# A two-stack transformer on one core: activations at other offsets to the weights in SBUF, and the forget decay of the keys added on VectorE instead of by a matmul

## The chip, the cores and the metric

The kernel runs on one core of a Trainium2 chip. The metric is the device time of one execution in microseconds (us), lower is better; the median of three executions is given. Five engines work side by side on the core: TensorE (PE, with its weight loads listed as PEld), VectorE (DVE), ScalarE (ACT), GpSimd (POOL) and SyncE (SP), which here only issues DMAs.

## The reference

256 tokens of width 1024 go through two stacks of two layers each. The first stack has three attention-like branches and a gated feed-forward network in each layer; the second has two feed-forward networks around a mixer. Nearly all of the arithmetic is `x @ w` with a weight matrix that is read once. The part of the reference beside these products that the change touches is the forgetting attention of the first stack:

```python
def forgetting_attention(q, k, v, f_logit):
    log_f = jax.nn.log_sigmoid(f_logit)
    cum = jnp.cumsum(log_f, axis=1).transpose(0, 2, 1)      # 4 heads x 256 tokens
    for blk in range(s // Q_BLOCK):                         # Q_BLOCK = 128
        ...
        logits = jnp.einsum('bihd,bjhd->bhij', q[:, q0:q1], k[:, :q1]) * d ** -0.5
        logits = logits + cum[:, :, q0:q1, None] - cum[:, :, None, :q1]
        mask = jnp.arange(q0, q1)[:, None] >= jnp.arange(q1)[None, :]
        p = jax.nn.softmax(jnp.where(mask, logits, -jnp.inf), axis=-1)
        ...
```

The term `- cum[:, :, None, :q1]` belongs to the key; it is the same for all queries.

## The kernel before, in words

The activations lie transposed, features on partitions and tokens along the free dimension, as 8 (or 22) blocks `k` of 128 features by 256 tokens. Every fp32 operand of a large product is split into a high and a low part (`hh`, `hl` for the activations, `wh`, `wl` for the weights), and `mm3` (lines 332 to 337) makes one product of three matmuls: `wh`·`hh`, `wh`·`hl` and `wl`·`hh`. The activations move, 256 columns long, and the 128x128 piece of the weights is loaded. In `kT` (line 354) the roles are exchanged. There are 15,600 of these matmuls.

`run` (line 259) takes the weights in the order of the program's steps: SP loads 512 KB into one of six `raw` tiles, ACT makes `wh` (line 289) and DVE makes `wl` (line 290) from half of it, four halves ahead of the matmuls. One half feeds twelve matmuls. The tiles `wh` and `wl` have ten buffers each of 2048 bytes per partition, and each starts at 128 modulo 256 bytes.

The activations lie as follows, as the program's addresses give it. The distance is the start of the activation operand less the start of the weight operand of the same matmul, modulo 256 bytes; it is the same for all blocks and for the high and the low tile, except where the table has a list.

| operand, where | matmuls | distance before |
|---|---|---|
| `hh`, `hl` (norm's output, xp pool) | 8,208 | 0 |
| `hidh`, `hidl` (hidden layer of a feed-forward network) | 3,168 | 128 |
| `bh`, `bl` where no norm is due (`norm_begin(None)`), rows of 258 tokens | 2,112 | 0, 8, ... 56 in `bh`, 64, 72, ... 120 in `bl`, by block |
| `brh`, `mxh`, `yh`, `ph` and their low parts | 1,248 | 128 |
| `bh`, `bl` in `first_pair` with a norm, 258 columns | 864 | 0 to 56 and 64 to 120, by block |

The forgetting attention: `small` (line 927) makes the cumulative sums `cum` of four heads as four rows and their negative `ncum`. Four units of the input projection later, `cores` (line 1157) flushes what is deferred and starts `fox(h)` for the four heads, five ticks apart (a tick is one block `k` of a large product). `fox` (line 950) writes the scores of two query blocks into PSUM with two plain fp32 matmuls, and adds `ncum` of its head to all rows with two more, whose loaded operand is one column of the identity matrix broadcast to 128 columns of four rows (`selh`). Each plain fp32 matmul shows as two records in the trace. DVE then adds the query's `cum` and the mask in one instruction for each query block (lines 960 and 961), and ACT and DVE make the softmax. Other work of PE goes on between the parts of `fox`.

Of the kernel before, what the change touches and what calls it, by code (L numbers as in the profile page):

```python
# [15 lines left out]
S = 256  # L16
# [5 lines left out]
NEG = -1e30  # L22
# [31 lines left out]
def _consts():  # L54
    f = np.float32
    ident = np.eye(128, dtype=f)
    half = 64
    inv = (f(10000.0) ** (-np.arange(half, dtype=f) / f(half))).astype(f)
    ang = (np.arange(S, dtype=f)[:, None] * inv[None, :]).astype(f)
    cos = np.cos(ang.astype(np.float64)).astype(f).T  # L60
    sin = np.sin(ang.astype(np.float64)).astype(f).T
    cosF = np.concatenate([cos, cos], 0)
    sinF = np.concatenate([-sin, sin], 0)
    i = np.arange(128)
    foxm = np.concatenate([np.zeros((128, 128), f),
                           np.where(i[:, None] >= i[None, :], 0.0, NEG).astype(f)], 1)
    u = ((i[:, None] > i[None, :]) & (i[:, None] // 64 == i[None, :] // 64)).astype(f)
    sel = (i[:, None] // 64 == np.arange(2)[None, :]).astype(f)
    t = np.arange(S)
    retd = []  # L70
    for h in range(4):
        lg = np.log1p(-np.exp2(-5.0 - h))
        d = np.exp(np.abs(t[:, None] - t[None, :]) * lg) * 128.0 ** -0.5
        d = np.where(t[:, None] // 64 <= t[None, :] // 64, d, 0.0).astype(f)
        retd += [d[:128], d[128:, 128:]]
    retd = np.concatenate(retd, 1)
    dist = np.abs(t[:, None] - t[None, :]).astype(f)
    ci, cj = t[:, None] // 64, t[None, :] // 64
# [113 lines left out]
class Prog:  # L192
# [6 lines left out]
    def __init__(self, ctx, tc, io, dbg=None):  # L199
        self.tc, self.nc, self.io, self.dbg = tc, tc.nc, io, dbg  # L200
        nc = self.nc
        self.V, self.A, self.G, self.PE = nc.vector, nc.scalar, nc.gpsimd, nc.tensor
        self.steps = []
        self.side = []
        pool = lambda name, **k: ctx.enter_context(tc.tile_pool(name=name, **k))
        self.cp = pool("cst", bufs=1)
        self.wp = pool("wts", bufs=self.WB)
        self.xp = pool("res", bufs=1)
        self.np_ = pool("nrm", bufs=2)
        self.tp = pool("tiny", bufs=4)  # L210
        self.dp = pool("dram", bufs=1, space=bass.MemoryType.DRAM)
        self.pg = pool("psg", bufs=4, space=PSUM)
        self.pm = pool("psm", bufs=4, space=PSUM)
        self.off, npar = _offsets()
        self.par = self.cp.tile([128, npar], F32, name="par")
        self.ident = self.cp.tile([128, 128], F32, name="ident")
        self.ones = self.cp.tile([128, 256], F32, name="ones")
        self.mhalf = self.cp.tile([128, 16], F32, name="mhalf")
        self.mod = [self.cp.tile([128, 48], F32, name=f"mod{l}") for l in range(2)]
        self.cact = self.np_.tile([128, D], F32, name="cact", tag="sy", bufs=1)  # L220
        self.gm = {}
        self.x = self.xp.tile([128, 8, S], F32, name="x")
        for k in (0, 4):
            self.dma(self.x[:, k:k + 4, :], io["xT"].rearrange("p (k t) -> p k t", t=S)[:, k:k + 4, :])
        self.dma(self.cact, io["cb"])
        self.dma(self.par, io["par"])
        self.dma(self.ident, io["c_id"])
        self.V.memset(self.ones, 1.0)
        self.V.memset(self.mhalf, -0.5)
        self.lam = self.cp.tile([128, 8], F32, name="lam")  # L230
        self.A.activation(self.lam[:, 0:1], self.mhalf[:, 0:1], AF.Silu)
        self.A.activation(self.cact, self.cact, AF.Silu)
# [179 lines left out]
    def norm_begin(self, kind, a=None, b=None):  # L412
# [4 lines left out]

        bh = self.xp.tile([128, 8, S + 2], F32R, name="bh", tag="bh")
        bl = self.xp.tile([128, 8, S + 2], F32R, name="bl", tag="bl")
        nk = {"kind": kind, "bh": bh, "bl": bl}  # L420
        if kind == "rms":
            base = 24 * b
# [17 lines left out]
                gains(o, 4)  # L440
        nk["gains"] = gains
        self.nk = nk

    def norm_add(self, mp, **k):
        with self.tc.high_priority():
# [81 lines left out]
    def norm_apply_(self):  # L527

        nk, V, A, x = self.nk, self.V, self.A, self.x
        bc = nk["bc"]  # L530
        hh = self.xp.tile([128, 8, S], F32R, name="hh", tag="hh")
        hl = self.xp.tile([128, 8, S], F32R, name="hl", tag="hl")
        qv, qa = self.queue(), self.queue(1)
        if nk["kind"] == "ln":
            parts = [slice(0, 1), slice(1, 2)] if 0 else [slice(0, 2)]
# [81 lines left out]
    def opening(self, units):  # L617


        def stats(ws):  # L620
            self.h = tuple(self.xp.tile([128, 8, S], F32R, name=n, tag=n) for n in ("hh", "hl"))
            g = self.tp.tile([128, 8], F32, name="gm", tag="gm")
            self.nk = {"kind": "rms", "bh": None, "bl": None, "g": g, "b": self.mod[0][:, 0:8]}
            for mp in range(4):
                self.norm_add(mp, split=False)
            self.norm_stats()
            self.norm_spread()
            self.opened = self.nk["spread"]
# [82 lines left out]
    def ffn_first(self, l, extra=()):  # L711
# [2 lines left out]
        st = {}  # L714

        def begin(ws):
            st["hh"] = self.st([128, KF, S], F32R, "hidh")
            st["hl"] = self.st([128, KF, S], F32R, "hidl")
        self.step([], begin)
        wc, bc = f"w_conv{l}", f"b_conv{l}"  # L720

# [51 lines left out]
    def ffn_second(self, l, f, j_ln):  # L773
# [1 line left out]
        st = {}  # L775

        def begin(ws):
            st["hh"] = self.st([128, KF, S], F32R, "hidh")
            st["hl"] = self.st([128, KF, S], F32R, "hidl")
        self.step([], begin)  # L780

        def evac_g(j):
# [87 lines left out]
    def mix(self, l, extra=()):  # L870
# [18 lines left out]
        self.step([], begin)  # L889

        def tables(ws):
            c = T([128, 898 + 1536], F32, "cmix")
            self.dma(c, self.io["c_mix"])
            b["cos"], b["sin"], b["foxm"] = c[:, 0:256], c[:, 256:512], c[:, 512:768]
            b["U"], b["sel"] = c[:, 768:896], c[:, 896:898]
            b["retd"] = c[:, 898:898 + 1536].rearrange("p (h c) -> p h c", h=4)
            a2 = T([128, 256], F32, "a2")
            self.dma(a2[32:49, :], self.io[f"a2{l}"][32:49, :])
            b["a2"] = a2


        def fox_qk(dst, u, gi):
            def fn(ps):
                if u == 0:
                    b[dst] = T([128, 4, S], F32, dst)
                n = self.st([128, 4, 128], F32, "w2", 4)
                r = self.head_rs(ps.rearrange("p t (h d) -> p (t h) d", h=2), 4, "hr")
                V.tensor_tensor(out=n, in0=ps.rearrange("p t (h d) -> p (t h) d", h=2),
                                in1=r[:, 0:4].unsqueeze(2).to_broadcast([128, 4, 128]), op=MULT)

                def turn():
                    pt = self.psM((128, 2, S))
# [14 lines left out]
        def small(ps):  # L927
# [8 lines left out]
            cum = z  # L936
            V.tensor_tensor_scan(out=cum[0:4, :], data0=self.ones[0:4, :], data1=lf[0:4, :], initial=0.0, op0=MULT, op1=ADD)
            V.tensor_scalar(lf[0:4, :], cum[0:4, :], -1.0, None, MULT)
            b["ncum"] = lf

            def turn():
                pt = self.psM()
# [4 lines left out]
                V.tensor_copy(out=b["cumT"], in_=pt[:, 0:8])  # L947
            self.defer(12, turn)

        def fox(h):  # L950
            q, k, v, m = b["qF"], b["kF"], b["fv"], b["foxm"]
            ps = self.psM((128, 2, S))
            mm = lambda o, l_, r_, s, e: PE.matmul(o, l_, r_, start=s, stop=e, skip_group_check=True)  # L953
            selh = self.ident[0:4, h:h + 1].to_broadcast([4, 128])
            for t in range(2):
                n = 128 * (t + 1)
                mm(ps[:, t, 0:n], q[:, h, t * 128:(t + 1) * 128], k[:, h, 0:n], t == 0, False)
                mm(ps[:, t, 0:n], selh, b["ncum"][0:4, 0:n], False, True)
            s = T([128, 384], F32, "sc", 2)
            V.scalar_tensor_tensor(s[:, 0:128], ps[:, 0, 0:128], b["cumT"][:, h:h + 1], m[:, 128:256], ADD, ADD)  # L960
            V.scalar_tensor_tensor(s[:, 128:384], ps[:, 1, :], b["cumT"][:, 4 + h:5 + h], m, ADD, ADD)
            nm = self.tiny(2, "nm")
            V.tensor_reduce(out=nm[:, 0:1], in_=s[:, 0:128], axis=AX.X, op=MAX, negate=True)
            V.tensor_reduce(out=nm[:, 1:2], in_=s[:, 128:384], axis=AX.X, op=MAX, negate=True)
# [191 lines left out]
            self.one(wi(5), keepT("fv", 1), "T")  # L1156
        def cores(ws):
            self.flush()
            self.spawn(gla_decay())
            for h in range(4):  # L1160
                self.spawn(fox(h), 5 * h)
            self.tick(0)
# [346 lines left out]
    def mixer_c(self, l):  # L1509
# [399 lines left out]
        def ybuf(ws):  # L1909
            while "cored" not in b:  # L1910
                self.tick()
            b["yh"] = self.xp.tile([128, 8, S], F32R, name="hh", tag="hh")
            b["yl"] = self.xp.tile([128, 8, S], F32R, name="hl", tag="hl")
            for hp in b["early"]:
                ysplit(hp)

# [73 lines left out]
```

## Time and profile before

| | |
|---|---|
| median of three runs (lowest to highest) | 2081.24 us (2081.13 to 2082.68) |
| the profiled execution | 2082.02 us |
| its span, first to last instruction | 2080.2 us |
| PE busy | 2033.9 us (98%) |
| DVE, ACT, POOL busy | 1534.7 us (74%), 1202.1 us (58%), 43.0 us (2%) |
| mean granted clock of PE | 0.997 of full speed |
| read from HBM | 397.32 MB |

Busy time of PE is the union of the matmuls' records. A record lasts some 280 ns and the next one begins after 120 ns, so records overlap, and "98%" does not tell how fast the matmuls follow each other. For that one counts the records in a stretch.

### The profile page before, as it was taken

The page shows a single profiled execution, that of the slowest core. Times are in us where ns is not written, and L with a number is a line of the kernel's source. Part 1 is how long each engine was busy: PE and PEld are TensorE (multiplying, and loading weights), DVE is VectorE, ACT ScalarE, POOL GpSimd, SP SyncE. Part 2 cuts the span into 40 slices and gives each one's busy share as a digit, 9 for nine tenths or more (in the row PEclk, how much of TensorE's full clock was granted, in tenths as well). Part 3 has the DMA queues.
Part 4 walks back from the last instruction along what each step waited for, and adds up shares of the span by engine and source line. Part 5 has one row for each costly group of instructions (what it writes and reads, how often), then busy time and mean ns, then how long its engine had stood idle before and what let it go on. Part 6 is the DMA issues. An engine that isn't in the chain of part 4 may idle for free.

```text
span 2080.2 us, 42885 instructions
## 1 busy us (share of the span) xinstructions
PE 2033.9 (98%) x16848; PEld 2006.6 (96%) x16848; DVE 1534.7 (74%) x2971; ACT 1202.1 (58%) x2255; POOL 43.0 (2%) x46
## 2 busy tenths in 40 slices
PE   7999999999999999999999999999999999899998
PEld 7999999999999999999999999999999998899998
DVE  8768989977669789765566898567755687586557
ACT  4755466566645467554555777556655586365545
POOL 0000000000000000000000000000000000000000
PEclk9999999999999999999999999999999999999999
DMA  9746977875447877666656346664656654246553
GB/s 340 248 121 199 322 250 243 293 239 193 144 156 245 277 243 243 193 178 189 186 180 190 127 131 208 184 180 156 211 184 180 180 156 127 62 147 200 179 168 103
DMA packets 123488, 403.40 MB, mean 194 GB/s; under 512 B 17010, under 2 KB 24468, under 8 KB 123028
## 3 DMA queue, kind: packets, MB, share of 16 engines
q1 hardware_dynamic: 112868, 397.24, 60.0%
q10 hardware_dynamic: 10416, 3.41, 0.6%
q8 instruction: 132, 2.16, 0.4%
q14 instruction: 72, 0.59, 0.1%
HBM read 397.32 MB, written 3.28 MB: 193 GB/s over the span
## 4 chain that ended last, share of the span: by engine, by line
PE 91%; DVE 5%; DMA 2%; issue 1%; POOL 1%; ACT 1%; DVEq 0%; ACTq 0%; POOLq 0%
PE psg L334 26%; PE psg L335 26%; PE psg L336 26%; PE psw L334 1%; PE psw L335 1%; PE psw L336 1%; DVE wl L290 1%; DMA raw<-w_ada 1%; PE psm L1687 1%; PE psm L953 1%; PE psm L1782 1%; DMA xx<-dx 1%; DMA dx<-xb 1%; PE psm L409 0%; PE psm L1084 0%
## 5 line engine op out<-in xcount | busy, mean ns | idle before, releaser
L289 ACT CAST wh<-raw 128x512 fp32r<-128x512 f32 x1304 | 783.7, 616 | 668.3 <-PE psg L335 467.6
L290 DVE TENSOR_TENSOR wl<-raw,wh 128x512 fp32r<-128x512 f32 x1304 | 871.9, 684 | 363.7 <-ACT wh L289 345.9
L334 PE MATMUL psg<-hh,wh 128*128 128x256 f32 x2328 | 661.8, 285 | 3.6 <-ACT wh L289 3.2
L335 PE MATMUL psg<-hl,wh 128*128 128x256 f32 x2328 | 661.5, 284 | 1.5 <-DVE hl L388 1.4
L336 PE MATMUL psg<-hh,wl 128*128 128x256 f32 x2328 | 661.0, 284 | 0.8 <-DVE wl L290 0.8
L334 PEld LDWEIGHTS psg<-hh,wh 128*128 128x128 f32 x2328 | 447.0, 192 | 5.8 <-ACT wh L289 3.5
L335 PEld LDWEIGHTS psg<-hl,wh 128*128 128x128 f32 x2328 | 447.9, 192 | 2.3 <-DVE hl L388 1.6
L336 PEld LDWEIGHTS psg<-hh,wl 128*128 128x128 f32 x2328 | 447.7, 192 | 1.5 <-DVE wl L290 1.0
L336 PE MATMUL psg<-hidh,wl 128*128 128x256 f32 x1056 | 297.3, 282 | 0.0
L335 PE MATMUL psg<-hidl,wh 128*128 128x256 f32 x1056 | 297.3, 282 | 0.0
L334 PE MATMUL psg<-hidh,wh 128*128 128x256 f32 x1056 | 297.3, 282 | 0.0
L334 PEld LDWEIGHTS psg<-hidh,wh 128*128 128x128 f32 x1056 | 198.9, 188 | 0.0
L335 PEld LDWEIGHTS psg<-hidl,wh 128*128 128x128 f32 x1056 | 198.8, 188 | 0.0
L336 PEld LDWEIGHTS psg<-hidh,wl 128*128 128x128 f32 x1056 | 198.8, 188 | 0.0
L335 PE MATMUL psg<-bl,wh 128*128 128x256 f32 x704 | 197.9, 281 | 0.0
L336 PE MATMUL psg<-bh,wl 128*128 128x256 f32 x704 | 197.8, 281 | 0.0
L334 PE MATMUL psg<-bh,wh 128*128 128x256 f32 x704 | 197.7, 281 | 0.0
L402 DVE CUSTOM_DVE_ANT_0 raw<-raw,cact,par 128x1024 f32<-128x1024 f32 x96 | 122.5, 1279 | 29.9 <-DMA raw<-w_ada 29.9
L335 PEld LDWEIGHTS psg<-bl,wh 128*128 128x128 f32 x704 | 132.8, 189 | 0.3 <-DVE bl L388 0.2
L334 PEld LDWEIGHTS psg<-bh,wh 128*128 128x128 f32 x704 | 132.8, 189 | 0.0
L336 PEld LDWEIGHTS psg<-bh,wl 128*128 128x128 f32 x704 | 132.6, 188 | 0.0
L334 PE MATMUL psg<-wh,hh 128*128 128x256 f32 (+1 forms) x336 | 97.7, 294 | 0.0
(446 smaller groups left out, 3004.7 us busy)
## 6 DMA issues: line engine op xcount, KB each, us to landing
raw<-f_up SPq DMA_DIRECT2D x176, 512.0 KB, 4.5
raw<-w_ada SPq DMA_DIRECT2D x96, 512.0 KB, 5.2
raw<-w_up SPq DMA_DIRECT2D x88, 512.0 KB, 5.1
raw<-f_dn SPq DMA_DIRECT2D x80, 512.0 KB, 3.7
raw<-w_in SPq DMA_DIRECT2D x66, 512.0 KB, 4.0
raw<-w_mg SPq DMA_DIRECT2D x46, 512.0 KB, 5.0
raw<-w_down SPq DMA_DIRECT2D x40, 512.0 KB, 4.2
raw<-c_in SPq DMA_DIRECT2D x32, 512.0 KB, 4.5
```

Of the source, the lines that this page charges most:

```text
L289: self.A.copy(out=wh[:, :e], in_=r)
L290: self.V.tensor_tensor(out=wl[:, :e], in0=r, in1=wh[:, :e].bitcast(F32), op=SUB)
L334: mm(ps, wh, xh, start=first, stop=False, skip_group_check=True)
L335: mm(ps, wh, xl, start=False, stop=False, skip_group_check=True)
L336: i = mm(ps, wl, xh, start=False, stop=last, skip_group_check=True)
L402: i = self.V.tensor_tensor_reduce(out=w, in0=w, in1=self.cact, scale=1.0, scalar=self.P(f"b_ada{l}", j), op0=MULT, op1=ADD, accum_out=self ...
L953: mm = lambda o, l_, r_, s, e: PE.matmul(o, l_, r_, start=s, stop=e, skip_group_check=True)
L1687: mm = lambda o, l_, r_, s: PE.matmul(o, l_, r_, start=s, stop=True, skip_group_check=True)
L1782: PE.matmul(p[:, i, :], l_(i, h), r_(i, h), start=(i == 0), stop=True, skip_group_check=True)
```

## The change

Two edits that don't depend on each other, and a small one.

1. The tiles `hh`/`hl` get 256 bytes more, `hidh`/`hidl` 512, and `pair_of` puts the data inside them at an offset from a table, one number for each stage. All distances are then the same for the high and the low tile. `bh`, `bl` without a norm are packed to rows of 256.

| stage, in order | operand | before | after |
|---|---|---|---|
| layer 0: mixing, then feed-forward | `hh` | 0 | 64, 192 |
| | `hid` | 128 | 192 |
| layer 1: mixing, then feed-forward | `hh` | 0 | 192, 224 |
| | `hid` | 128 | 224 |
| second stack, layer 0 | packed `bh`, `bl` | 0 to 120, mixed | 0 and 64 |
| | `hid` (two networks) | 128 | 64, 160 |
| | `hh` (mixer, second network, gate) | 0 | 64, 32, 192 |
| second stack, layer 1 | packed `bh`, `bl` | 0 to 120, mixed | 0 and 64 |
| | `hid` (two networks) | 128 | 32, 96 |
| | `hh` (mixer in, mixer out, second network, gate) | 0 | 160, 64, 128, 64 |

Four of the `hh` stages (the feed-forward ones) have 960 matmuls each, every `hid` stage has 528.

2. `ncum` is written to DRAM by POOL's queue (4x256) and read back spread over 128 partitions (128x1024, 512 KB). Ahead of `fox`, `fox_bias` adds the mask to it, one half in a tile `nb0`, one half in place. `fox` leaves out its two matmuls with `selh`, and DVE adds the prepared tile where it added the mask. The table `c_mix` shrinks by 128 columns.

```diff
+        self.places = [b // 4 for b in (64, 192, 192, 224, 64, 32, 192, 160, 64, 128, 64)]
+        self.hid_places = [b // 4 for b in (64, 96, 192, 32, 160, 224)]
...
+        if kind is None:
+            bh, bl = (t.rearrange("p k t -> p (k t)")[:, 0:8 * S].rearrange("p (k t) -> p k t", t=S) for t in (bh, bl))
...
+    def pair_of(self, pool, tag, kt, extra, at):
+
+        out = []
+        for n in (tag + "h", tag + "l"):
+            t = pool.tile([128, kt * S + extra], F32R, name=n, tag=n, bufs=1)
+            out.append(t[:, at:at + kt * S].rearrange("p (k t) -> p k t", t=S))
+        return tuple(out)
+
+    def normed(self):
+
+        return self.pair_of(self.xp, "h", 8, 64, self.places.pop(0))
...
-        hh = self.xp.tile([128, 8, S], F32R, name="hh", tag="hh")
-        hl = self.xp.tile([128, 8, S], F32R, name="hl", tag="hl")
+        hh, hl = self.normed()
...
-            st["hh"] = self.st([128, KF, S], F32R, "hidh")
-            st["hl"] = self.st([128, KF, S], F32R, "hidl")
+            st["hh"], st["hl"] = self.pair_of(self.sp, "hid", KF, 128, self.hid_places.pop(0))
...
-            b["ncum"] = lf
+            nd = self.dp.tile([4, S], F32, name=f"nd{l}")
+            nb = b["nb"] = T([128, 4, S], F32, "sall")
+            self.nc.gpsimd.dma_start(out=nd, in_=lf[0:4, :])
+            self.nc.gpsimd.dma_start(out=nb, in_=nd.unsqueeze(0).to_broadcast([128, 4, S]))
...
+        def fox_bias():
+
+            m = b["foxm"].unsqueeze(1).to_broadcast([128, 4, 128])
+            b["nb0"] = T([128, 4, 128], F32, "w2", 4)
+            with self.tc.issue_after(b["normed"]):
+                V.tensor_tensor(out=b["nb0"], in0=b["nb"][:, :, 0:128], in1=m, op=ADD)
+            with self.tc.issue_after(b["normed"]):
+                V.tensor_tensor(out=b["nb"][:, :, 128:256], in0=b["nb"][:, :, 128:256], in1=m, op=ADD)
...
-            selh = self.ident[0:4, h:h + 1].to_broadcast([4, 128])
             for t in range(2):
                 n = 128 * (t + 1)
-                mm(ps[:, t, 0:n], q[:, h, t * 128:(t + 1) * 128], k[:, h, 0:n], t == 0, False)
-                mm(ps[:, t, 0:n], selh, b["ncum"][0:4, 0:n], False, True)
+                mm(ps[:, t, 0:n], q[:, h, t * 128:(t + 1) * 128], k[:, h, 0:n], t == 0, True)
             s = T([128, 384], F32, "sc", 2)
-            V.scalar_tensor_tensor(s[:, 0:128], ps[:, 0, 0:128], b["cumT"][:, h:h + 1], m[:, 128:256], ADD, ADD)
-            V.scalar_tensor_tensor(s[:, 128:384], ps[:, 1, :], b["cumT"][:, 4 + h:5 + h], m, ADD, ADD)
+            V.scalar_tensor_tensor(s[:, 0:128], ps[:, 0, 0:128], b["cumT"][:, h:h + 1], b["nb0"][:, h, :], ADD, ADD)
+            V.scalar_tensor_tensor(s[:, 128:384], ps[:, 1, :], b["cumT"][:, 4 + h:5 + h], b["nb"][:, h, :], ADD, ADD)
...
         def cores(ws):
             self.flush()
+            fox_bias()
```

PE where the first `fox` of layer 0 begins, before (`a` holds `ncum`, `ident` is the identity matrix):

```order
L993 MATMUL psm<-a_825,ffz 128x256 x2
L953 MATMUL psm<-kF,qF 128x128
L953 MATMUL psm<-a_825,ident 128x128
L953 MATMUL psm<-kF,qF 128x256
L953 MATMUL psm<-a_825,ident 128x256
L336 MATMUL psg<-hh,wl 128x256
```

and after (line numbers are those of the changed kernel):

```order
L1016 MATMUL psm<-a_825,ffz 128x256 x2
L978 MATMUL psm<-kF,qF 128x128
L978 MATMUL psm<-kF,qF 128x256
L337 MATMUL psg<-hh,wl 128x256
```

The two matmuls with the identity are gone at all eight places; nothing else moves on PE.

DVE at the same place, before (L908 normalises the last keys, L290 makes the weights' low parts, L960 and L961 begin the softmax):

```order
L908 TENSOR_TENSOR w_1207<-psg,hr 128x512
L290 TENSOR_TENSOR wl<-raw,wh 128x512 x2
L960 SCALAR_TENSOR_TENSOR sc<-psm,cumT,cmix 128x128
L961 SCALAR_TENSOR_TENSOR sc<-psm,cumT,cmix 128x256
```

and after:

```order
L920 TENSOR_TENSOR w_1211<-psg,hr 128x512
L971 TENSOR_TENSOR w_1233<-sall,cmix 128x512
L973 TENSOR_TENSOR sall<-sall,cmix 128x4x128
L291 TENSOR_TENSOR wl<-raw,wh 128x512 x2
L983 SCALAR_TENSOR_TENSOR sc<-psm,cumT,w_1233 128x128
L984 SCALAR_TENSOR_TENSOR sc<-psm,cumT,sall 128x256
```

The two new additions stand ahead of two halves of weights. In layer 1 they stand behind one half more, and seven follow them ahead of the first softmax.

POOL in layer 1, after (L395 is the power behind each `head_rs`; before, the four powers stand in a row with no DMA among them):

```order
L395 TENSOR_TENSOR hr<-hv,mhalf 128x4 x2
L954 DMA nd_6930<-a_6714 4x256
L395 TENSOR_TENSOR hr<-hv,mhalf 128x4
L955 DMA sall<-nd_6930 128x1024
L395 TENSOR_TENSOR hr<-hv,mhalf 128x4
```

The second DMA, which needs the first one's data, stands ahead of the power for the last keys. In layer 0 both DMAs stand ahead of all four powers.

## Rows read from the trace of the kernel before

**Rows 1.** The page: busy time by engine, and the chain by engine.
```profile
PE 2033.9 (98%) x16848; PEld 2006.6 (96%) x16848; DVE 1534.7 (74%) x2971; ACT 1202.1 (58%) x2255; POOL 43.0 (2%) x46
...
PE 91%; DVE 5%; DMA 2%; issue 1%; POOL 1%; ACT 1%; DVEq 0%; ACTq 0%; POOLq 0%
```

**Rows 2.** Stretches of one kind: length, PE's busy time and records, clock, DMA.
```profile
core 0: us, PE busy (x), PEclk, DMA share, GB/s
800.00:890.00 90.00, 90.00 (x752) 1.00 0.70 225
900.00:955.00 55.00, 55.00 (x466) 1.00 0.63 191
970.00:1080.00 110.00, 110.00 (x929) 1.00 0.62 187
```

**Rows 3.** The page's groups: line, engine, tiles, forms, count, busy us, mean ns.
```profile
L334 PE MATMUL psg<-hh,wh 128*128 128x256 f32 x2328 | 661.8, 285 | 3.6 <-ACT wh L289 3.2
...
L336 PE MATMUL psg<-hidh,wl 128*128 128x256 f32 x1056 | 297.3, 282 | 0.0
...
L335 PE MATMUL psg<-bl,wh 128*128 128x256 f32 x704 | 197.9, 281 | 0.0
```

**Rows 4.** PE in order of time, just behind small matmuls: start and length, us.
```profile
584.77 0.28 PE L335 MATMUL psg<-wl,hh 128*128 128x256 f32 x1
...
585.24 0.28 PE L336 MATMUL psg<-wh,hl 128*128 128x256 f32 x1
...
586.26 0.28 PE L335 MATMUL psg<-wl,hh 128*128 128x256 f32 x1
...
586.72 0.28 PE L336 MATMUL psg<-wh,hl 128*128 128x256 f32 x1
```

**Rows 5.** PE in order of time, one unit with rows of 258.
```profile
1005.39 0.28 PE L334 MATMUL psg<-bh,wh 128*128 128x256 f32 x1
...
1006.10 0.28 PE L334 MATMUL psg<-bh,wh 128*128 128x256 f32 x1
...
1011.09 0.28 PE L334 MATMUL psg<-bh,wh 128*128 128x256 f32 x1
```

**Rows 6.** PE at the first `fox` in order of time, and line 953's records.
```profile
97.59 0.48 PE L953 MATMUL psm<-a,ident 4*128 4x128 f32 x2
98.00 0.70 PE L953 MATMUL psm<-kF,qF 128*128 128x256 f32 x2
98.63 0.69 PE L953 MATMUL psm<-a,ident 4*128 4x256 f32 x2
99.25 0.39 PE L336 MATMUL psg<-hh,wl 128*128 128x256 f32 x1
...
L953 PE MATMUL psm<-a,ident x32: 270/373/478, 97.6 to 563.9; 4*128 4x128 f32 x16, 4*128 4x256 f32 x16
```

**Rows 7.** DVE in order of time, layers 0 and 1: `ncum` to first softmax.
```profile
73.27 0.28 DVE L938 TENSOR_SCALAR a<-ffz 4x256 f32<-4x256 f32 x1
...
94.78 0.69 DVE L908 TENSOR_TENSOR w<-psg,hr 128x512 f32<-128x512 f32 x1 [1.12 <-POOL hr L394]
...
99.36 0.35 DVE L960 SCALAR_TENSOR_TENSOR sc<-psm,cumT,cmix 128x128 f32<-128x128 f32 x1 [2.69 <-PE psm L953]
...
524.64 0.28 DVE L938 TENSOR_SCALAR a<-ffz 4x256 f32<-4x256 f32 x1
...
532.53 0.69 DVE L908 TENSOR_TENSOR w<-psg,hr 128x512 f32<-128x512 f32 x1 [1.18 <-POOL hr L394]
...
544.24 0.35 DVE L960 SCALAR_TENSOR_TENSOR sc<-psm,cumT,cmix 128x128 f32<-128x128 f32 x1 [1.31 <-PE psm L953]
```

**Rows 8.** DMA issues by tile: engine, count, KB each, median us to landing.
```profile
dl<-lt ACTq DMA_DIRECT2D x4, 256.0 KB, 3.0
...
xx<-dx ACTq DMA_DIRECT2D x2, 512.0 KB, 6.1
```

More of the change, by code (lines that the diff above doesn't have):

```diff
@@ L64, in _consts @@
     i = np.arange(128)
-    foxm = np.concatenate([np.zeros((128, 128), f),
-                           np.where(i[:, None] >= i[None, :], 0.0, NEG).astype(f)], 1)
+    foxm = np.where(i[:, None] >= i[None, :], 0.0, NEG).astype(f)
     u = ((i[:, None] > i[None, :]) & (i[:, None] // 64 == i[None, :] // 64)).astype(f)
@@ L620, in stats @@
         def stats(ws):
-            self.h = tuple(self.xp.tile([128, 8, S], F32R, name=n, tag=n) for n in ("hh", "hl"))
+            self.h = self.normed()
             g = self.tp.tile([128, 8], F32, name="gm", tag="gm")
@@ L777, in begin @@
         def begin(ws):
-            st["hh"] = self.st([128, KF, S], F32R, "hidh")
-            st["hl"] = self.st([128, KF, S], F32R, "hidl")
+            st["hh"], st["hl"] = self.pair_of(self.sp, "hid", KF, 128, self.hid_places.pop(0))
         self.step([], begin)
@@ L891, in tables @@
         def tables(ws):
-            c = T([128, 898 + 1536], F32, "cmix")
+            c = T([128, 770 + 1536], F32, "cmix")
             self.dma(c, self.io["c_mix"])
-            b["cos"], b["sin"], b["foxm"] = c[:, 0:256], c[:, 256:512], c[:, 512:768]
-            b["U"], b["sel"] = c[:, 768:896], c[:, 896:898]
-            b["retd"] = c[:, 898:898 + 1536].rearrange("p (h c) -> p h c", h=4)
+            b["cos"], b["sin"], b["foxm"] = c[:, 0:256], c[:, 256:512], c[:, 512:640]
+            b["U"], b["sel"] = c[:, 640:768], c[:, 768:770]
+            b["retd"] = c[:, 770:770 + 1536].rearrange("p (h c) -> p h c", h=4)
             a2 = T([128, 256], F32, "a2")
@@ L907, in fn @@
                 r = self.head_rs(ps.rearrange("p t (h d) -> p (t h) d", h=2), 4, "hr")
-                V.tensor_tensor(out=n, in0=ps.rearrange("p t (h d) -> p (t h) d", h=2),
-                                in1=r[:, 0:4].unsqueeze(2).to_broadcast([128, 4, 128]), op=MULT)
+                i = V.tensor_tensor(out=n, in0=ps.rearrange("p t (h d) -> p (t h) d", h=2),
+                                    in1=r[:, 0:4].unsqueeze(2).to_broadcast([128, 4, 128]), op=MULT)
+                b["normed"] = getattr(i, "ins", i)
                 def turn():
@@ L948, in small @@
             self.defer(12, turn)
+        def fox_bias():
[5 more added lines that the diff above has]
+                V.tensor_tensor(out=b["nb"][:, :, 128:256], in0=b["nb"][:, :, 128:256], in1=m, op=ADD)
         def fox(h):
-            q, k, v, m = b["qF"], b["kF"], b["fv"], b["foxm"]
+            q, k, v = b["qF"], b["kF"], b["fv"]
             ps = self.psM((128, 2, S))
             mm = lambda o, l_, r_, s, e: PE.matmul(o, l_, r_, start=s, stop=e, skip_group_check=True)
-            selh = self.ident[0:4, h:h + 1].to_broadcast([4, 128])
             for t in range(2):
                 n = 128 * (t + 1)
-                mm(ps[:, t, 0:n], q[:, h, t * 128:(t + 1) * 128], k[:, h, 0:n], t == 0, False)
-                mm(ps[:, t, 0:n], selh, b["ncum"][0:4, 0:n], False, True)
+                mm(ps[:, t, 0:n], q[:, h, t * 128:(t + 1) * 128], k[:, h, 0:n], t == 0, True)
             s = T([128, 384], F32, "sc", 2)
-            V.scalar_tensor_tensor(s[:, 0:128], ps[:, 0, 0:128], b["cumT"][:, h:h + 1], m[:, 128:256], ADD, ADD)
-            V.scalar_tensor_tensor(s[:, 128:384], ps[:, 1, :], b["cumT"][:, 4 + h:5 + h], m, ADD, ADD)
+            V.scalar_tensor_tensor(s[:, 0:128], ps[:, 0, 0:128], b["cumT"][:, h:h + 1], b["nb0"][:, h, :], ADD, ADD)
+            V.scalar_tensor_tensor(s[:, 128:384], ps[:, 1, :], b["cumT"][:, 4 + h:5 + h], b["nb"][:, h, :], ADD, ADD)
             nm = self.tiny(2, "nm")
@@ L1911, in ybuf @@
                 self.tick()
-            b["yh"] = self.xp.tile([128, 8, S], F32R, name="hh", tag="hh")
-            b["yl"] = self.xp.tile([128, 8, S], F32R, name="hl", tag="hl")
+            b["yh"], b["yl"] = self.normed()
             for hp in b["early"]:
```

## The prediction

> **What bounds the kernel now.** I read the page's busy times and chain first, then stretches of one kind, then the rows around the forgetting attention. PE is busy for 98% of the span, and the chain that ended last is 91% PE and 5% DVE [rows 1]. So a nanosecond saved on PE is nearly always a nanosecond of the end, and what DVE, ACT or POOL save or spend counts only where PE waits for them.
>
> Busy time hides the pace, since a record of 281 to 285 ns [rows 3] overlaps the next two. I count instead: in a stretch without waits the records, less the 2.4 whose tails only reach in (283 / 119), give the time of one. With `hh` moving (800 to 890 us) it is 90 / (752 - 2.4) = 120.1 ns. With `hidh`/`hidl` (900 to 955 us) it is 55 / (466 - 2.4) = 118.6 ns. With `bh`/`bl` in rows of 258 (970 to 1080 us) it is 110 / (929 - 2.4) = 118.7 ns [rows 2]. The granted clock is 1.00, the 2.4 GHz level, in all three, the form is the same 128*128 128x256 in all three [rows 3], and DMA load is about the same. What differs is where the moving operand lies: 0, 128, and a mix of 0 to 120 bytes from the weights. The slowest distance is the one with most of the matmuls, and the change leaves it in all of its stages.
>
> **The change part by part.**
>
> Decay of the keys. PE loses the pairs of records of `a,ident`: 98.00 - 97.59 = 0.41 us and 99.25 - 98.63 = 0.62 us, together 1.03 us for one head [rows 6]. There are 32 records, 4 for each of 8 heads [rows 6], so 8 x 1.03 = 8.2 us, all on PE and none of them behind another engine: **-8.2 us**.
>
> What replaces them lies elsewhere. DVE gets two additions of 128x512 in each layer, which I take at the 0.69 us of the normalisation of that size [rows 7]: 4 x 0.69 = 2.8 us of DVE. In layer 0 DVE sat idle for 2.69 us ahead of the first softmax [rows 7], and two additions are 1.4 us; the two halves of weights that now come 1.4 us later stand ahead of that idle time too. In layer 1 the idle time just ahead of it is 1.31 us [rows 7], and DVE had waited for ACT's halves before that. Cost 0; without that cover, 2.8 us.
>
> The spread has to land before the first addition, or DVE stops with all that is queued behind it: the low parts of the weights, the softmax, and with them PE. No row shows a DMA from POOL's queue. The nearest are 256 KB to DRAM in 3.0 us and 512 KB back in 6.1 us, both from ACT's queue [rows 8]: 9.1 us for the two, one behind the other. Layer 0: 73.55 + 9.1 = 82.7 us, and the addition is due at 95.5 us. Layer 1: 524.92 + 9.1 = 534.0 us, and it is due behind 532.53 + 0.69 and one half of weights (0.7), at 533.9 us [rows 7]. So it is level there; the halves that are four ahead (12 x 120 ns = 1.4 us each) cover a few us of delay. I take 0, and 0 to 3 us for the range. On POOL the power for the last keys stands behind the second DMA, which waits some 3 us for the first: 524.92 + 3.0 = 527.9 us, while that power's result is used at 532.53 us [rows 7]. Cost 0.
>
> Pace with `hh`. The `hh`,`wh` group has 2,328 records, and two more groups have as many [rows 3]: 6,984 matmuls at 120.0 ns. (Some 1,200 with the roles exchanged or into other PSUM tiles I leave out; they are often interrupted.) No row shows the new distances with both tiles alike, 128 excepted, which is 118.6 ns and which one of the four feed-forward stages takes. Bounds for the others: upwards nothing excludes the 120.1 of distance 0; downwards, the matmuls right behind a group of small ones take 585.24 - 584.77 = 0.47 and 586.72 - 586.26 = 0.46 us for four, 116 ns [rows 4]. The mixed stage is the nearest look at several distances: one unit of 48 takes 1011.09 - 1005.39 = 5.70 us, 118.75 ns, and its first block of six, at distances 0 and 64, 1006.10 - 1005.39 = 0.71 us, 118.3 ns [rows 5]. Half of the blocks there are off by 8 bytes from a multiple of 16, which the change ends. I take 118.3: 6,984 x 1.7 = **-11.9 us**; at the ends, 0 and 6,984 x 4 = -28.
>
> Pace with `hid`. 3 x 1,056 = 3,168 matmuls [rows 3] leave a known 118.6 for unknown distances: at 118.3, **-1.0 us**; at the ends +4.4 (120.0) and -8.2 (116).
>
> Pace with packed `bh`, `bl`. 3 x 704 = 2,112 [rows 3] become all like the first block of six: (118.7 - 118.3) x 2,112 = **-0.8 us**; ends +2.7 and -5.7.
>
> Behind a faster PE the weights come late next. ACT and DVE are at 58% and 74% [rows 1], and the DMA share is 0.62 to 0.70 in the long stretches [rows 2], so 1% more pace finds them ready. Cost 0.
>
> Sum: 8.2 + 11.9 + 1.0 + 0.8 = 21.9 us. The profiled execution's 2082.0 us (a span of 2080.2 and 1.8 around it) becomes 2060.1; the median of the runs is 0.8 lower than the profiled one, so 2059.3. I say **2059 us**.
>
> **The rivals.**
>
> *Distance does nothing for the pace.* 120 and 118.6 could belong to the tiles for another reason, say what ACT and DVE do in those stages, and stay with them. Then only the matmuls of the decay go: 2081.2 - 8.2 = 2073 us. For it: no row has `hh` at another distance. Against it: the same clock, form and DMA load, and the steady 120.1 over 750 records, which work on ACT and DVE would scatter. The Trainium skill is on this rival's side (SBUF — State Buffer, Who interferes with whom): TensorE has one read port for the moving operand and one for weight loads, and "PE and ACT never wait on anyone". By that rule the places make no difference and the time is this rival's. The trace's 120.1 against 118.6 says that the rule isn't the whole of it.
>
> *The new distances are much better than any now held for long.* At the 116 ns of rows 4 the sum is 8.2 + 28 + 8.2 + 5.7 = 50 us: 2031 us; half way, at 117, it is 8.2 + 21 + 5.1 + 3.6 = 38 us: 2043 us. For it: the hardware does follow at 116 when the loads have just got ahead. Against it: within a few matmuls it falls back, and no whole stage holds it.
>
> *The new distances are worse, and the time ends above today's.* 12,264 matmuls move, which now take 6,984 x 120.0 + 3,168 x 118.6 + 2,112 x 118.7 = 1,464.5 us. The 8.2 us of the decay are eaten when the mean rises above (1,464.5 + 8.2) / 12,264 = 120.08 ns; at 121 it is 11.3 us slower than before, 2092 us. For it: `hid` leaves a known distance, and at one like 0 it alone gives back 4.4 us. Against it: 120.1 is the slowest stage of the trace.
>
> *A late spread.* If a DMA from POOL's queue takes twice the time of rows 8, it lands 9 us late in layer 1, of which the halves ahead cover some 3; 2059 + 6 = 2065 us. Within the range.
>
> **How the numbers follow.** Forecast, pace of 117.5 to 119.2 at the new places, late spread included: 0.62, 2047 to 2070 us. Much better: 0.20, down to 2031. Distance does nothing: 0.12, 2073. Worse: 0.06, of which 0.03 ends within 0.2% of now. The range leaves out the worse case and the lower half of the better one: 2038 to 2074 us. A change below 0.2% (4.2 us) can't be told from none by this measurement. Faster by more: 0.62 + 0.20 + 0.12 = 0.94 (the rival without pace still gains 8); same 0.03; slower 0.03.
>
> **What would show it.** Line 978 in the changed kernel has 32 records instead of 64, and the four behind `ident` are gone. In a stretch of a feed-forward network 750 records take about 88.7 us where they took 90; the stage at distance 128 takes 118.6 ns a matmul as `hid` does now. If `hh` stays at 120 everywhere, the first rival holds; if `hid` goes up, the third. DVE's first addition in layer 1 should show no wait for the spread above a few us, and PE none for the low parts of the weights behind it. The forecast is wrong if the stages with the same work but other distances differ by more than 2 ns, since then one value for all of them was the wrong way to count.

## The result and the profile after

The changed kernel takes 2058.6 us (median of 4 runs, 2055.4 to 2061.5) where the one before, on the same chip, takes 2081.2: a ratio of 0.9885, 95% interval 0.9863 to 0.9906. The forecast was 2059, within 2038 to 2074. The total came out as predicted; the way to it did not.

The page of after, the same two lines as [rows 1]:

```profile
PE 2001.0 (97%) x16816; PEld 1977.4 (96%) x16816; DVE 1534.2 (75%) x2975; ACT 1198.5 (58%) x2255; POOL 45.7 (2%) x50
...
PE 85%; DVE 7%; DMA 4%; ACT 2%; issue 2%; POOL 1%; DVEq 0%; SPq 0%; ACTq 0%; POOLq 0%
```

PE lost 32.9 us of busy time (2033.9 to 2001.0), but the span only 25.9 (2080.2 to 2054.3). PE's share of the chain fell from 91% to 85%, while DVE's rose from 5% to 7% and DMA's from 2% to 4%: more of the end now hangs on waits for them. So more was gained on PE than the 21.9 us predicted, and some of it was given back.

A long stretch is a stage in which the same kind of product runs on without a break: four `hh` stages of 960 matmuls, six `hid` stages of 528, two packed `bh`, `bl` stages of 1,056. Windows inside them, in after (as [rows 2]: length, PE's busy time and records, clock, DMA). First `hh` at distances 192, 224, 32 and 128, then the two packed stages, then `hid` at 192, 224, 64, 32 and 96 (the one at 160 is left out):

```profile
310.00:400.00 90.00, 90.00 (x797) 1.00 0.82 274
770.00:860.00 90.00, 90.00 (x763) 1.00 0.71 232
1240.00:1330.00 90.00, 90.00 (x774) 1.00 0.64 205
1845.00:1935.00 90.00, 90.00 (x761) 1.00 0.63 191
950.00:1040.00 90.00, 90.00 (x752) 1.00 0.58 185
1450.00:1540.00 90.00, 90.00 (x767) 1.00 0.65 209
425.00:470.00 45.00, 45.00 (x398) 1.00 0.74 241
890.00:935.00 45.00, 45.00 (x383) 1.00 0.60 185
1075.00:1120.00 45.00, 45.00 (x385) 1.00 0.62 188
1570.00:1615.00 45.00, 45.00 (x388) 1.00 0.62 190
1960.00:2005.00 45.00, 45.00 (x377) 1.00 0.55 157
```

The count is what to read. By the prediction's formula, 797 records in 90 us are 113.3 ns a matmul, 774 are 116.6, 763 118.3, 761 118.6, and 752 are the 120.1 of before. All windows have the clock at 1.00. One kind of work has paces from 113 to 120. The first packed stage runs at 120.1 and the second at 117.7, with the same distances, 0 and 64, in both. The last `hid` stage, at 96, became slower (118.7 to 120.0).

To sum up, I took the time of each stretch, from its first matmul to the next stretch's, in both traces, and the mean interval of its undisturbed matmuls, from their starts. The differences by pace alone: `hh` -25.7 us (the four feed-forward stages -6.4, -1.6, -3.2, -1.3; the mixing and the branches -13.2), `hid` -3.7, packed `bh`/`bl` +0.1. With the -8.4 of the decay (below) that is -37.7. The span moved by -25.9, so **11.8 us were given back**, in few places: 4.0 behind the mixing of layer 0, 5.0 in the branches of layer 1, 1.5 in the stage behind the second half's first mixer, the rest in small pieces. In that last stage the waits listed for PE are the same in both traces (2.3 and 0.5 us), but in after the granted clock falls to 0.50 there for 3.4 us, and in before it doesn't.

The largest of these, 4.0 us, where the first block of the feed-forward network starts. PE in order of time in after, then windows with the busy time of PE, PEld, DVE, ACT and POOL, the clock, and the DMA's share and rate:

```profile
293.26 0.29 PE L337 MATMUL psw<-bh,wl 128*128 128x258 f32 x1
296.29 1.01 PE L510 MATMUL psm<-ones,sq 128*128 128x1 f32 x4 [2.74 <-DVE sq L498]
297.17 0.56 PE L335 MATMUL psw<-bh,wh 128*128 128x258 f32 x1
297.53 0.42 PE L336 MATMUL psw<-bl,wh 128*128 128x258 f32 x1
297.74 0.42 PE L337 MATMUL psw<-bh,wl 128*128 128x258 f32 x1
```

```profile
293.50:296.30 2.80, 0.06 (x2) 0.01 (x1) 2.80 (x8) 2.46 (x5) 0.00 (x0) 0.90 0.93 360
297.20:300.00 2.80, 2.80 (x14) 2.80 (x15) 2.19 (x5) 0.66 (x2) 1.67 (x1) 0.50 0.65 164
```

The same place in before:

```profile
302.57 0.61 PE L495 MATMUL psm<-ones,sq 128*128 128x1 f32 x4 [1.53 <-DVE sq L483]
...
302.50:306.00 3.50, 3.43 (x28) 3.43 (x29) 3.50 (x8) 1.24 (x2) 1.67 (x1) 1.00 0.47 88
```

The squares for the norm come from DVE, which is busy for all of those 2.80 us. PE, which now arrives earlier, waits 2.74 us for them instead of 1.53. Behind that wait the granted clock is 0.50, the 1.2 GHz level, and the matmuls start 0.21 us apart (297.53 to 297.74) instead of 0.12, for some 5 us: 1.2 us of longer wait and 2.8 us of slow clock. In the branches of layer 1 (670 to 735 us) PE waits in two groups (total us, times, longest), where before has 0.3 us for the gate and nothing for the low parts:

```profile
PE psg L337 <- DVE wl L291: 2.1, 2, 1.2
PE psg L335 <- DVE gate L1247: 1.7, 2, 1.1
```

DVE itself stands there for the DMA of `w_ada`, and a low part that PE needs is made behind that wait:

```profile
702.67 1.29 DVE L403 CUSTOM_DVE_ANT_0 raw<-raw,cact,par 128x1024 f32<-128x1024 f32 x1 [3.21 <-DMA raw<-w_ada]
703.88 0.69 DVE L291 TENSOR_TENSOR wl<-raw,wh 128x512 fp32r<-128x512 f32 x1
704.63 0.39 PE L337 MATMUL psg<-hh,wl 128*128 128x256 f32 x1 [1.21 <-DVE wl L291]
```

Before has these waits for `w_ada` too: 19.2 us in seven of them over all branches of layer 1 (657 to 765 us), 21.6 in seven in after (640 to 745 us). They grew by 2.4 us, and PE now comes early enough to meet them; no run separates the two.

### The profile page after: what moved, and what is told of

Read it like the earlier page. It is cut to its first block, busy times and chain, and to the rows that moved or that the text cites. A ratio compares the mean times of both kernels' runs of the same rounds, so it can differ in the third digit from the quotient of the medians.

```text
span 2054.3 us, 42838 instructions
## 1 busy us (share of the span) xinstructions
PE 2001.0 (97%) x16816; PEld 1977.4 (96%) x16816; DVE 1534.2 (75%) x2975; ACT 1198.5 (58%) x2255; POOL 45.7 (2%) x50
## 4 chain that ended last, share of the span: by engine, by line
PE 85%; DVE 7%; DMA 4%; ACT 2%; issue 2%; POOL 1%; DVEq 0%; SPq 0%; ACTq 0%; POOLq 0%
PE psg L335 25%; PE psg L336 24%; PE psg L337 24%; DVE wl L291 2%; DMA raw<-w_ada 2%; PE psw L335 1%; PE psw L336 1%; PE psw L337 1%; PE psm L1711 1%; PE psm L1806 1%; DMA xx<-dx 1%; DVE raw L403 0%; PE psm L410 0%; PE psm L1107 0%; PE psm L335 0%
## 5 line engine op out<-in xcount | busy, mean ns | idle before, releaser
L290 ACT CAST wh<-raw 128x512 fp32r<-128x512 f32 x1304 | 781.1, 616 | 636.8 <-PE psg L336 447.4
L335 PE MATMUL psg<-hh,wh 128*128 128x256 f32 x2328 | 652.9, 281 | 5.0 <-ACT wh L290 3.2
L337 PE MATMUL psg<-hh,wl 128*128 128x256 f32 x2328 | 651.3, 280 | 3.3 <-DVE wl L291 3.3
L336 PE MATMUL psg<-hl,wh 128*128 128x256 f32 x2328 | 651.7, 280 | 1.5 <-DVE hl L389 1.4
L335 PEld LDWEIGHTS psg<-hh,wh 128*128 128x128 f32 x2328 | 437.7, 188 | 6.6 <-ACT wh L290 5.6
L337 PEld LDWEIGHTS psg<-hh,wl 128*128 128x128 f32 x2328 | 438.2, 188 | 4.1 <-DVE wl L291 3.9
L336 PEld LDWEIGHTS psg<-hl,wh 128*128 128x128 f32 x2328 | 438.3, 188 | 2.4 <-DVE hl L389 1.6
```

What stands on the lines that cost most here:

```text
L290: self.A.copy(out=wh[:, :e], in_=r)
L335: mm(ps, wh, xh, start=first, stop=False, skip_group_check=True)
L336: mm(ps, wh, xl, start=False, stop=False, skip_group_check=True)
L337: i = mm(ps, wl, xh, start=False, stop=last, skip_group_check=True)
```

## The experiments

**The decay alone.** After, with the operands back at their old places:

```diff
-        hh, hl = self.normed()
+        hh = self.xp.tile([128, 8, S], F32R, name="hh", tag="hh")
+        hl = self.xp.tile([128, 8, S], F32R, name="hl", tag="hl")
...
```

`yh`/`yl` and `hidh`/`hidl` go back in the same way, and `bh`/`bl` have rows of 258 everywhere.

> The kernel after with all activation operands back at their old distances; only the forget decay stays changed. The prediction: 32 pairs of records gone and nothing behind them, -8.2 us, so 2073 us, with 120.0 ns a matmul in the stretches with hh and 118.7 with hidh. Rival (part of the saved time is not PE's, since in the profile of after the two stretches that hold the attention lose only 2.6 and 3.7 us beyond what their pace explains): -6.3 us, so 2075 us. If the places moved by the decay's buffers mattered, the paces would differ from 120.0 and 118.7.

2074.4 us (9 runs, 2072.8 to 2078.1), ratio 0.9962 (0.9949 to 0.9975). Where [rows 2] have 752, 90 us hold

```profile
800.00:890.00 90.00, 90.00 (x753) 1.00 0.69 221
```

so the pace is as before. The two stretches with the attention lose 3.7 and 4.7 us, 8.4 together, where I had 8.2. But 2.1 us are given back behind the mixing of layer 0, at the wait for the squares, and 1.5 later; 1.3 are gained in two short pieces of layer 1, and 0.4 lost behind the last stage. This execution's span falls by 5.7 in all (2080.2 to 2074.5), while the median falls by 8.2 (2082.5 to 2074.4). The total alone can't tell 8.2 from the rival's 6.3, since its interval is 5.2 to 10.6 us; the two stretches can, and there the prediction's term holds. The 2.1 us are also a sign that the loss at the squares comes with PE's earlier arrival, as no activation has moved here: PE waits 2.1 us for them instead of 1.5, and the clock then falls to 0.50 for 3.4 us.

**Move the weights, not the activations.** Before, with one 64-byte constant moved from ahead of the weights to behind them:

```diff
-        self.mhalf = self.cp.tile([128, 16], F32, name="mhalf")
+        self.mhalf = self.xp.tile([128, 16], F32, name="mhalf")
```

> The kernel before with the small constant of 64 bytes moved from ahead of the weights to behind them: every weight lies 64 bytes lower and no activation moves, so hh lies at 64 instead of 0 and hidh at 192 instead of 128; the decay is as before. Theory (the distance alone sets the pace): the four feed-forward stages with hh run at 117.8 ns as after's stretches at 64 do, and hidh at 113.4 to 113.7: 3,840 x 2.2 + 3,168 x 5.0 = 24 us less, and with the other stages some 27 less: 2050 to 2058 us. Rival (the place of the activation in memory, or the tile, or what runs beside it sets the pace): hh stays at 120.0, hidh at 118.7, and the time at 2081 us.

2059.8 us (2057.5 to 2064.6), ratio 0.9896 (0.9872 to 0.9919), 2 us above the theory's range: as much as the whole change, with no activation moved and the decay as before. Windows of `hh` at 64 (two) and `hid` at 192 (two):

```profile
320.00:400.00 80.00, 80.00 (x708) 1.00 0.86 288
780.00:860.00 80.00, 80.00 (x681) 1.00 0.73 238
890.00:935.00 45.00, 45.00 (x384) 1.00 0.61 183
1080.00:1125.00 45.00, 45.00 (x400) 1.00 0.65 196
```

That is 113.4 and 117.9 ns for `hh`, 117.9 and 113.2 for `hid`. The rival falls: no activation moved, so it is not the activation's place alone that matters, and the paces are those that after and the kernels below have at 64 and 192. The distance sorts them all, within a limit: only two places of the weights were tried, and no period other than 256 bytes. Yet my theory is only half right: 64 and 192 both give two paces, 113.3 and 117.8.

**192 everywhere, twice.** The tables of places changed:

```diff
-        self.places = [b // 4 for b in (64, 192, 192, 224, 64, 32, 192, 160, 64, 128, 64)]
-        self.hid_places = [b // 4 for b in (64, 96, 192, 32, 160, 224)]
+        self.places = [b // 4 for b in (192, 192, 192, 192, 192, 192, 192, 192, 192, 192, 192)]
+        self.hid_places = [b // 4 for b in (64, 64, 64, 64, 64, 64)]
```

> The kernel after with hh and hidh at distance 192 in every stage. Theory (distance sets the pace, and 192 gives 113.4 wherever hh or hidh moves): the three feed-forward stages that were at 224, 32 and 128 lose (5.0 + 3.3 + 5.3) x 960 = 13 us, the five hidh stages that were elsewhere lose 24.2 ns in all x 528 = 12.8 us, so 26 us less than after if nothing comes late: 2033 us; waits for weights and statistics gave back 6 to 10 us of 29 in after, and as much more here makes 2033 to 2041. Rival (113 and 118 are two states into which a stage falls by chance): paces differ between stages with the same distance, and the time lies at 2045 to 2060 us.

2036.0 us (2028.2 to 2039.7), ratio 0.9770 (0.9737 to 0.9803). In its profile eight of the ten long stretches run at 113.3 to 113.6 ns, and two neighbours at 117.8; here `hh` at 770 and at 1235 us:

```profile
770.00:860.00 90.00, 90.00 (x797) 1.00 0.72 236
...
1235.00:1325.00 90.00, 90.00 (x767) 1.00 0.66 212
```

> The kernel with hh and hidh at 192 once more, unchanged. In its first profile ten stretches at the same distance ran at 113.4 ns and two neighbours (hh and hidh of the first feed-forward network behind the mixing of the second half) at 117.8. Theory (113.4 and 117.8 are two states of one distance, and which one a stretch gets is settled by chance when the stream starts again after an interruption): the slow stretches are others this time, or there are none, and the time lies anywhere in 2028 to 2040 us. Rival (something fixed at that place in the program, such as the banks or what runs beside it, makes 117.8): the same two stretches are slow again, and the time is 2036 us.

2035.9 us, and the same two stretches are slow again (767 records from 1235 us). So it is not plain chance. But this time the first of them began at 113.5 ns, and changed to 117.8 where one matmul came 0.06 us late:

```profile
1231.53 0.28 PE L336 MATMUL psg<-hl,wh 128*128 128x256 f32 x1
1231.65 0.34 PE L337 MATMUL psg<-hh,wl 128*128 128x256 f32 x1
1231.82 0.28 PE L335 MATMUL psg<-hh,wh 128*128 128x256 f32 x1
```

**A map of distances.** The same tables with a value of its own for each long stretch, and in a second kernel exchanged between `hh` and `hid`:

> The kernel after with another distance in each long stretch: hh of the four feed-forward networks at 16, 48, 80, 112, hidh of the six stages at 144, 176, 208, 240, 184, 200. Theory (the pace is a function of the distance, with a steep optimum near 192): 176 to 208 run at 113 to 116 ns, the far side at 117 to 120. Rival (only multiples of 64 matter): all of them run at one pace, about 118 to 120. Both would make the time 2055 to 2070 us.

> The kernel after with the distances of the first map exchanged between hh and hidh: hh of the four feed-forward networks at 144, 176, 208, 240, hidh of the six stages at 16, 48, 80, 112, 8, 72. Theory (a distance allows a few paces whichever tile moves): hidh at 16 gives 118.7 and at 48 and 80 118.3 as hh did, at 112 113.4, hh at 144 118.7, at 176 and 208 119.2, at 240 117.2. Rival (tile, stage or chance decide): hidh at 112 or hh at 240 differ from these by more than 1 ns. The time is 2055 to 2062 us in either case.

2054.2 and 2058.6 us (one run each). From the first, `hh` at 16 and 112 and `hid` at 184; from the second, `hid` at 112 and 72:

```profile
310.00:400.00 90.00, 90.00 (x761) 1.00 0.84 287
1845.00:1935.00 90.00, 90.00 (x797) 1.00 0.63 197
1570.00:1615.00 45.00, 45.00 (x377) 1.00 0.62 189
```

```profile
1360.00:1405.00 45.00, 45.00 (x399) 1.00 0.59 171
1960.00:2005.00 45.00, 45.00 (x374) 1.00 0.55 161
```

All distances seen in long stretches, in ns a matmul (two numbers where two paces were seen):

| distance | 0 | 8 | 16 | 32 | 48 | 64 | 72 | 80 | 96 | 112 |
|---|---|---|---|---|---|---|---|---|---|---|
| ns | 120.0 | 116.7 | 118.7 | 116.7 | 118.3 | 113.3, 117.8 | 121.1 | 118.3 | 120.0 | 113.4 |

| distance | 128 | 144 | 160 | 176 | 184 | 192 | 200 | 208 | 224 | 240 |
|---|---|---|---|---|---|---|---|---|---|---|
| ns | 118.7 | 118.7 | 118.7 | 119.3 | 120.0 | 113.3, 117.8 | 120.0 | 119.2 | 118.3 | 117.2 |

Each of the eight distances measured with both tiles (16, 48, 80, 112, 144, 176, 208, 240) gave the same within 0.1 ns with `hh` and `hid`. My steep optimum around 192 fell: 184 and 200 are as bad as 0, and 112 is as good as 192.

**Interruptions.** After with 192, and small matmuls put in:

```diff
...
+        self.calls = getattr(self, "calls", 0) + 1
+        if self.calls % 64 == 0:
+            p = self.psM()
+            for _ in range(4):
+                mm(p[:, 0:1], self.ones[:, 0:128], self.ones[:, 0:1], start=True, stop=True, skip_group_check=True)
         mm(ps, wh, xh, start=first, stop=False, skip_group_check=True)
```

> The kernel with hh and hidh at 192, and four extra matmuls of one column into another PSUM tile ahead of every 64th triple (191 interruptions that compute nothing that is used). Theory (an interruption draws the state anew): within one feed-forward stretch of 960, stretches of 192 matmuls at 113.3 stand beside stretches at 117.8, and the mean lies between. Rival (the state belongs to the stretch): all five pieces of a stretch run at the same pace. Each interruption costs 0.3 to 0.6 us, so the time is 2036 + 57 to 115 = 2093 to 2150 us, plus some 15 us if half of the pieces are slow.

2087.3 us; the trace has 81 groups of four (648 records, two for each small matmul), not the 191 expected. Windows between two groups, in one `hh` stretch behind eighteen small matmuls in a row, and in the same stretch behind two more:

```profile
350.90:373.30 22.40, 22.40 (x200) 1.00 0.89 297
1260.00:1350.00 90.00, 90.00 (x767) 1.00 0.66 201
1361.00:1382.00 21.00, 21.00 (x188) 1.00 0.66 190
```

Both theories fall. Behind each of the 28 groups of four that stand inside a long stretch at 192 the pace was 113.3, nearly always as ahead of it, so it is not drawn anew by lot; and the stretch at 117.8 went to 113.3 right behind two small matmuls, so the pace isn't the stretch's own either. The packed stages, still at 0 and 64, have two paces as well: in the second, 117.8 ahead of two small matmuls (at 1524 us) and 120.1 behind them.

I then put `br`, `mx`, `p`, `yh` and the packed `bh`, `bl` at 192 too (other paddings of `hh`, `bl`; `hid` and the small ones follow), and that kernel with one and with four small matmuls at 17 places:

> The kernel after with hh, hidh, the packed bh and bl, and the small operands of the branches (br, mx, y, p) all at distance 192; only the rows of 258 stay mixed. Theory (the distance gives the pace): the two packed stretches go from 117.8 or 120.0 to 113.4, (118.9 - 113.4) x 2,112 = 11.6 us, and the small operands from 118.7 to 113.4 for 1,200 matmuls, 6 us: 2036 - 17 = 2019 us, up to 2030 when some stretches fall into 117.8 or waits give time back. Rival (bh and bl have another limit than their place): the packed stretches stay at 118 to 120 and the time at 2030 to 2036 us.

2039.1 us, and the runs lie between 2016.7 and 2053.8 with a granted clock of 0.992 to 0.994 in each, so the clock doesn't make the spread. The profiled one (2021.2 us) has both packed stages at 113.3 to 113.5, so the packed rows have no other limit; its first `hh` stretch, and `hid` behind it, are the slow ones this time (windows of the first two `hh` stretches and of the first packed stage):

```profile
310.00:400.00 90.00, 90.00 (x767) 1.00 0.82 275
770.00:860.00 90.00, 90.00 (x796) 1.00 0.71 233
945.00:1035.00 90.00, 90.00 (x796) 1.00 0.61 198
```

> The kernel with everything at 192, and one extra fp32 matmul of one column ahead of the fourth unit of each long stretch (17 in all, unused results). In the kernel with four such matmuls every 64 triples each of them was followed by 113.3 ns a matmul, whatever stood before. Theory (the small fp32 matmul leaves the stream in the fast state each time): 113.3 in the long stretches, 17 x 0.25 = 4 us for the extra work, 2017 to 2026 us with the runs within 10 us of each other. Rival (an interruption draws the state by chance): the runs spread over 2020 to 2055 us as they did without, with a median near 2040.

> The same with four small matmuls at each of the 17 places instead of one, which took 0.9 us each in the interrupted kernel. Theory: 113.3 in the long stretches, 2019 + 15 = 2034 us, runs within 10 us. If four settle the state and one doesn't, this one's runs lie close together and the other's don't. Rival (chance): the runs spread over 30 us or more, median near 2050.

2040.9 us (2035.8 to 2051.8) with one, 2042.6 (2038.4 to 2047.0) with four, where the theories had 2017 to 2026 and 2034. Ahead of and behind one small matmul, in the first `hh` stretch:

```profile
315.00:334.00 19.00, 19.00 (x170) 1.00 0.72 230
336.00:416.00 80.00, 80.00 (x681) 1.00 0.90 313
```

and ahead of and behind four, in the second:

```profile
766.00:794.00 28.00, 28.00 (x240) 1.00 0.60 182
796.00:876.00 80.00, 80.00 (x709) 1.00 0.72 233
```

One takes the stream from 113.4 to 117.9, four take it from 117.8 to 113.2. In all, one led to 117.8 in 4 of 4 cases inside a stretch of `hh` or packed `bh` (three of them from 113.3), and to 113.3 in 4 of 4 with `hid` (all from 117.8); four led to 113.3 in 8 of 8 (two from 117.8). Twelve in a row, where the groups of three places stood together, were followed by 117.8, and three in a row by 113.3. So the pace that follows goes with the number of small matmuls and with the stream that they interrupt. What in them decides is open, and that the runs differ because their waits differ is likely but not shown, as only one run of each kernel has a trace. As a remedy neither kernel helps: the median is no better than without, though with four the runs lie closer.

**112 everywhere.** The tables set to 112 (240 in the table of `hid`), then packed `bh`, `bl` there as well:

> The kernel after with hh and hidh at 112 in every stage. In the maps hh at 112 ran at 113.4 ns in the one stretch that had it and hidh at 112 in the one that had it. Theory (112 has the fast pace as its only one): 113.4 in all ten long stretches, 2036 us, and the runs within 5 us. Rival (112 has a second, slower state, as 64 and 192 have): some of the stretches run at 117 to 120 and the time lies at 2040 to 2060 us.

2030.8 us (2029.0 to 2033.8), ratio 0.9749 (0.9730 to 0.9768). All ten long stretches of `hh` and `hid` run at 113.3 to 113.7 ns, with waits and slow clocks ahead of some of them.

```diff
...
+        w = S if kind is None else S + 2
+        bh, bl = (self.xp.tile([128, 8 * (S + 2) + x], F32R, name=n, tag=n)[:, at:at + 8 * w].rearrange("p (k t) -> p k t", t=w)
+                  for n, x, at in (("bh", 16, 28 if kind is None else 0), ("bl", 48, 60 if kind is None else 0)))
...
```

> The kernel with hh and hidh at 112, and the packed bh and bl at 112 too (the constant of ones loses half its columns to make room, and the scan over the gates takes its ones from a scratch tile). The two packed stretches ran at 119.99 and 117.82 with bh at 0 and bl at 64. Theory (112 has 113.4 as its only pace, for every tile): they take (120.0 - 113.4) + (117.8 - 113.4) = 11 ns less for 1,056 matmuls each time, 11.6 us: 2030.8 - 11.6 = 2019 us, runs within 6 us of each other. Rival (two tiles with packed rows don't share the property): the two stretches stay at 117.8 or 120.0 and the time at 2028 to 2034 us, or the runs spread as they did with everything at 192 (2017 to 2054).

2023.3 us (2020.0 to 2023.8), ratio 0.9709 (0.9695 to 0.9722), the best of all by median and faster than both kernels. The packed stages, 752 and 767 records in after:

```profile
945.00:1035.00 90.00, 90.00 (x797) 1.00 0.63 198
...
1440.00:1530.00 90.00, 90.00 (x797) 1.00 0.62 195
```

The theory holds for moving activations, 4 us above its number: of the 24 long stretches at 112 in four kernels none had another pace, and the runs lie within 4 us of each other. No small matmuls were put into a kernel at 112.

It does not hold where the roles are exchanged, as in `kT`, and the weights move past loaded activations. In the mixing of layer 1 of this same kernel 96 such matmuls follow each other at the same places, the first and the last being

```profile
490.61 0.28 PE L335 MATMUL psg<-wh,hh 128*128 128x256 f32 x1
...
502.00 0.28 PE L337 MATMUL psg<-wh,hl 128*128 128x256 f32 x1
```

That is 11.39 / 95 = 119.9 ns, as slow as in before at 0 (119.8), while 192 gives 117.8 in the same place. Counted the other way round the distance is 256 - 112 = 144, for which the table has 118.7. So the table is one for moving activations alone.

## Why the prediction was right, and where it was not

**The decay: right.** 32 records are left at line 978, and those with the identity are gone. PE at the first head (where [rows 6] have four pieces), and DVE in layer 1:

```profile
95.11 0.92 PE L978 MATMUL psm<-kF,qF 128*128 128x128 f32 x4
...
97.41 0.82 PE L978 MATMUL psm<-kF,qF 128*128 128x128 f32 x4
```

```profile
523.68 0.69 DVE L971 TENSOR_TENSOR w<-sall,cmix 128x512 f32<-128x512 f32 x1 [1.76 <-DMA sall<-nd]
```

The additions take the 0.69 us of [rows 7]. The spread came late in layer 1, as feared, its two DMAs landing 3.6 and 6.2 us after issue where I had 9.1 together: DVE stood for 1.76 us, and the halves ahead covered it, since the only wait listed for PE from 515 to 545 us is 0.9 us for ACT's copy of the probabilities. Cost 0 holds.

**One pace for all new distances: wrong,** by the prediction's own test. The stages differ by 6.7 ns, not by less than 2. 118.3 was read from a stage that mixed distances and from six matmuls [rows 5]; the places are a set of separate paces, and `hh` got -25.7 us, not -11.9; `hid` got -3.7, not -1.0, and the packed rows +0.1, not -0.8. The rival of much better distances (it had 116) holds for some stages, with 113.3, the rival of worse ones for two (`hid` at 96, the first packed stage), and the stage at 128 takes 118.6 as said.

**"Behind a faster PE the weights come late next. Cost 0": wrong** by 11.8 us. I looked at DVE's mean share of 74% and at the DMA in the long stretches; the losses are in the short ones between. At the squares, which are no weights and which the term left out, DVE is busy for the whole 2.80 us; in the branches of layer 1 it stands for `w_ada`; and in two places the slow clock adds its price, which no term had. This term was 12 us too small, and the gain by pace 16 us (29.3 measured, 13.7 predicted): the two nearly cancel, and that is why the total was right. Nothing in the kernel makes them equal, so that was luck: the sum came out, two of its terms did not.

**The rival without an effect of distance: refuted** by moving the weights alone, -22.7 us. It stood on the Trainium skill (SBUF — State Buffer, Who interferes with whom), by which PE never waits on anyone; the runs here do not agree: with the same loads, forms and clock, 64 bytes of shift move `hid` from 118.7 to 113.2 or 117.9 ns. Why the distance matters is not shown.

## What to carry to other kernels

Where a stream of matmuls is the bound and each has its own weights, compute the distance of the two operands from the program's addresses, measure the pace of a few distances in one kernel with a value for each stage, and take one that has a single pace rather than the one with the best single run. Measure anew where the roles of the operands are exchanged. Count what a faster engine will reach earlier in the short stages between the long ones, by the busy time of the other engines there and not by their mean. A total that fits is no proof of its terms: check each by a window.

## What the hardware showed that was not expected

The paces are few: 113.3, 116.7, 117.8, 118.3, 118.7 and 120.0 ns come back at several distances, which at 2.4 GHz are 272, 280, 282.7, 284, 284.8 and 288 cycles; four distances have paces of their own (117.2 at 240, 119.2 and 119.3 at 208 and 176, 121.1 at 72). A stream can keep its pace for a whole stretch of 528 to 1,056 matmuls, and at 192 a hiccup of 0.06 us was followed by another; at 112 none of the waits that occurred was. That fits a kernel with everything at 192 having the fastest single run (2016.7 us) and a spread of 37 us. Why just these distances are good, and what selects the pace at 192, no run here settles.

The wait for the squares was followed by the 1.2 GHz level in after, and not in before; the price of 2.8 us was more than the 1.2 us of the longer wait.
